# Two decoder layers on one core: statistics' matmuls at fixed places of TensorE's order, six convolution taps emitted per chunk, freer transposes, and x's second half on another queue

## The chip, the core and the metric

The kernel runs on one NeuronCore of a Trainium2 chip. The metric is the time of one execution in device microseconds. A core has five engines that each work through a list of instructions in order and meet at semaphores: TensorE (PE, matrix products), VectorE (DVE), ScalarE (ACT), GpSimd (POOL) and SyncE (SP), which here only issues DMAs. TensorE and the others exchange results through PSUM, whose tiles are few.

## What is computed

Two layers; each runs a convolution branch and an attention branch on the same x (256 rows of 1024), merges them and normalizes. Shortened from the reference (with 256 rows and blocks of 256 the attention is plain causal attention):

```python
def hybrid_layer(x, w_in, b_in, conv_w, conv_b, cln_g, cln_b, w_pw2,
                 w_proj_a, w_proj_b, w_out, ln_g, ln_b, positions):
    u = x @ w_in + b_in
    a_val, a_glu, a_z, q, k, v, b_z, g_a, g_b = jnp.split(u, SPLIT_POINTS, axis=-1)
    h_a = conformer_conv(a_val, a_glu, conv_w, conv_b, cln_g, cln_b, w_pw2) * jax.nn.silu(a_z)
    y_a = h_a @ w_proj_a
    ...
    o = moba_attention(rope(q), rope(k), v)
    y_b = (o * jax.nn.silu(b_z)) @ w_proj_b
    merged = jax.nn.sigmoid(g_a) * y_a + jax.nn.sigmoid(g_b) * y_b
    out = merged @ w_out
    return layer_norm(DEEPNORM_ALPHA * x + out, ln_g, ln_b)

def conformer_conv(...):
    h = a_val * jax.nn.sigmoid(a_glu)
    # causal, one filter of 31 taps for each channel
    h = lax.conv_general_dilated(h, conv_w, ...) + conv_b
    h = jax.nn.silu(layer_norm(h, cln_g, cln_b))
    return h @ w_pw2
```

## The kernel before

**Weights and chunks.** The weights of a layer come in blocks of 256 columns (1 MB each) in the order of STREAM: V, then A_GLU and A_VAL in turn, B_Z, then MID (Q, K and G_A in turn for j = 0 to 3, then four times G_B), A_Z, PB, PW2, PA and WO, four blocks each. `load_w` issues their DMAs on SP's queue. `split_w` cuts a block into a rounded part hi (ScalarE, L120) and a rest lo (mostly GpSimd, L124). `gemm_a` computes two chunks of 128 output columns for a block: for each, eight matmuls of 512 columns with hi against x's own hi and lo parts (L176), and eight of 256 columns with lo (L174). A chunk's result lies in a PSUM tile of the pool `mmp`, which has three; ScalarE adds the bias to one half (L182) and VectorE adds the halves (L187). For Q and K the second chunk is added into the first one's tile, and VectorE's rope (L430 to L434) reads that tile, whose last reader is the addition L434.

**Convolution.** Its 31 taps for each of eight channel groups are 248 instructions a layer on VectorE, each a multiply and add into a PSUM accumulator (L373 for the first tap, L377 for the others). They wait in a list; after each chunk, `background(nconv[0])` emits NCV of them, with a lower priority, into the scheduler, which decides where they stand in VectorE's order. After the last tap of a group the group is added into a fold (L382).

**The convolution's norm.** `cln_mu` is a matmul of ones with the fold (cmu, L536), then VectorE subtracts the mean (L539) and ScalarE squares (L540). `cln_var` folds the squares (L527 to L529), has a matmul of ones (cvar, L545) and builds the factor r; `cln_b` makes from it, group by group, the input hc of PW2 (L558 to L562). `hook_az` calls cln_mu after chunk CM = 3 of A_Z and cln_var after chunk CV = 7; `ev_pb` calls cln_b along the chunks of PB, by the table CB.

**The boundary of the layers.** `part` is the product with WO, and V's in layer 1; `out_ln` normalizes 128 rows with `rstd`, whose VectorE instructions on 128x1 values are L221 to L225; `out_tr` transposes the new x (L652, two groups of four, one PSUM bank each) and splits it into hi (L654, ScalarE) and lo (L655, VectorE). The hook in `part` puts the first `out_tr` between the last matmuls of WO.

**What sets the order.** DMA queues run in order of issue. The Tile scheduler orders each engine's instructions by dependencies and priorities. Under `manual_schedule` TensorE's order is that of the code; this is so in MID, and from the last part of WO in layer 0 to the end of V in layer 1.

Of the kernel before, what the change touches and what calls it, by code (L numbers as in the profile page):

```python
# [10 lines left out]
F32 = mybir.dt.float32  # L11
# [3 lines left out]
AF = mybir.ActivationFunctionType  # L15
ALU = mybir.AluOpType
# [6 lines left out]
P = 128  # L23
KT = D // P
# [6 lines left out]
CW = 256  # L31
# [1 line left out]
EARLY = 6  # L33
NH2 = 2
CM = 3.0
CV = 7.0
CB = [[], [0], [1, 2], [3, 4], [5, 6], [7], [], []]
KE = 7
KN = 5
# [4 lines left out]
HP = 0  # L44
LATE = 150
LAG = 3
NCV = 4

A_VAL, A_GLU, A_Z, Q, K, V, B_Z, G_A, G_B, PW2, PA, PB, WO = range(13)
ORDER = [(V, j) for j in range(4)]  # L50
# [20 lines left out]
def decoder_trunk(ctx: ExitStack, tc: tile.TileContext, a, out):  # L71
    nc = tc.nc
# [3 lines left out]
    rawp = ctx.enter_context(tc.tile_pool(name="rawp", bufs=3))  # L76
# [11 lines left out]
    def u_f32(name, shape=(P, KT, S)):  # L88
        return unit.tile(list(shape), F32, tag="u", name=name)

    def u_pair(name):

        both = pair.tile([P, KT, 2, S], F32R, tag="p", name=name)
        return both[:, :, 0, :], both[:, :, 1, :], both

    def load_w(i):
        l, b, j = STREAM[i]
        raw = rawp.tile([P, KT, CW], F32, tag="raw", name=f"raw{i}")
        n = {1: 4, 2: 2}.get(i, 1)
        for q in range(n):  # L100
            ks = slice(q * KT // n, (q + 1) * KT // n)
            nc.sync.dma_start(out=raw[:, ks, :], in_=a["w"][i, :, ks, :])
        return raw

    W = {}
    raws = {}
# [43 lines left out]

    nconv = [NCV]
    pcs = [None]
# [43 lines left out]
    def wide(w):  # L196

        return w.rearrange("p (k h) c -> p k (h c)", h=2)

    def part(o, lhs, w, t, kh, late_x=False, cols=slice(0, 512), ks=range(4), hook=None):  # L200
        wh, wl = (wide(n) for n in w)
        xh, xl = lhs
        ts = slice(t * P, t * P + P)
        if late_x:
            seq = [(k, q) for q in (0, 2, 1) for k in ks]
        else:
            seq = [(k, q) for k in ks for q in (0, 1)] + [(k, 2) for k in ks]
        for n, (k, q) in enumerate(seq):
            kk = 4 * kh + k
            nc.tensor.matmul(o, (xl if q == 1 else xh)[:, kk, ts], (wl if q == 2 else wh)[:, k, cols],  # L210
                             start=(kk == 0 and n == 0), stop=(kh == 1 and n == len(seq) - 1))
            if hook is not None and n == 7:
                hook()

    def rstd(mv, name, fast):
        v = small.tile([P, 1], F32, tag="var", name="var" + name)
        y = small.tile([P, 1], F32, tag="ry", name="ry" + name)
        u = small.tile([P, 1], F32, tag="ru", name="ru" + name)
        if not fast:
            nc.scalar.activation(u, mv, AF.Sqrt, bias=eps)  # L220
            nc.vector.tensor_scalar(v, mv, EPS, None, op0=ALU.add)  # L221
            nc.vector.reciprocal(y, u)
            nc.vector.scalar_tensor_tensor(u, y, v, y, op0=ALU.mult, op1=ALU.mult)
            nc.vector.tensor_scalar(u, u, -0.5, 1.5, op0=ALU.mult, op1=ALU.add)
            nc.vector.tensor_tensor(y, y, u, op=ALU.mult)  # L225
            return y
        nc.gpsimd.tensor_scalar(v, mv, EPS, -0.5, op0=ALU.add, op1=ALU.mult)
        nc.scalar.activation(u, mv, AF.Sqrt, bias=eps)
        nc.vector.reciprocal(y, u)
        nc.scalar.activation(u, y, AF.Square)  # L230
        nc.scalar.activation(u, u, AF.Identity, scale=v, bias=oneh)
        nc.scalar.activation(y, y, AF.Copy, scale=u)
        return y

    xh, xl, xp = u_pair("x0")
    xf = u_f32("xf0")
    raw = rawp.tile([P, KT, CW], F32, tag="raw", name="raw0")
# [12 lines left out]
    for k in range(4):  # L250
        nc.sync.dma_start(out=raw4[:, k, :], in_=a["w"][0, :, 2 * k : 2 * k + 2, :])
        nc.scalar.dma_start(out=xf[:, k, :], in_=a["xT"][:, k, :])
    for k in (4, 6):
        nc.scalar.dma_start(out=xf[:, k : k + 2, :], in_=a["xT"][:, k : k + 2, :])

    def split_x(k0, k1):
        ks = slice(k0, k1)
# [4 lines left out]
    for k in range(NH2, 4):  # L262
        ks = slice(2 * k, 2 * k + 2)
# [35 lines left out]
    for l in range(DEPTH):  # L299
# [6 lines left out]
        x, xb = (xh, xl), xp  # L306

        v = u_f32(f"v{l}", (P, 2, D))
# [4 lines left out]
        if l == 0:  # L313
            for n in range(2):
# [5 lines left out]
                for kh in range(2):  # L320
                    w = next_w()
# [21 lines left out]
            ident, ones, mask, rt = load_consts()  # L343
# [74 lines left out]
        og, ol, op_ = u_pair(f"og{l}")  # L418
# [90 lines left out]
        for n, (b, j) in enumerate(MID):  # L509
            def hook(c, n=n):  # L510
                with tc.high_priority(offset=HP):
                    for f, p in plan.get(2 * n + c, []):
                        f(p)
# [28 lines left out]
        def cln_var():  # L542
            f = fold(cln["sq"], cln["sq"])
            vp = cvp.tile([P, 2, S], F32, tag="cv", name=f"cvar{l}")
            nc.tensor.matmul(vp[:, 0, :], ones, f, start=True, stop=True)  # L545
            u = tmp.tile([P, S], F32, tag="g", bufs=2, name=f"cu{l}")
            y = vp[:, 1, :]
            nc.scalar.activation(u, vp[:, 0, :], AF.Sqrt, bias=eps)
            nc.vector.reciprocal(y, u)
            nc.scalar.activation(u, y, AF.Square)  # L550
            nc.vector.tensor_scalar(vp[:, 0, :], vp[:, 0, :], EPS, None, op0=ALU.add)
            nc.vector.scalar_tensor_tensor(u, u, -0.5, vp[:, 0, :], op0=ALU.mult, op1=ALU.mult)
            nc.vector.scalar_tensor_tensor(y, u, 1.5, y, op0=ALU.add, op1=ALU.mult)
            cln["r"] = y
# [8 lines left out]

        def ev_pb(ct, o):
            nc.vector.scalar_tensor_tensor(gb[:, ct, :], gb[:, ct, :], 1.0, o, op0=ALU.add, op1=ALU.mult)
            if ct == 0:
                hc.extend(u_pair(f"hc{l}"))
            for q in CB[ct]:
                cln_b(q)

        def hook_az(c, j):
            if 2 * j + c == CM:
                background(len(conv_ops))
                cln_mu()
            if 2 * j + c == CV:
                cln_var()

        for j in range(4):
            gemm_a(xb, ev_az, lambda c, j=j: hook_az(c, j))
        for j in range(4):  # L580
            gemm_a(op_, ev_pb)

        rows = load_rows(l)
        if l == 0:
# [25 lines left out]
        xn = xs  # L610
        if not last:
            xh, xl, xp = u_pair(f"x{l + 1}")
# [33 lines left out]

        def out_tr(t):
            xt = sp.tile([P, 2, 512], F32, tag="s", name=f"xt{l}_{t}")
            for g in range(2):
                tp = xt[:, g, :].rearrange("p (i q) -> p i q", i=4)  # L650
                for i in range(4):
                    nc.tensor.transpose(tp[:, i, :], xn[:, t, 512 * g + i * P : 512 * g + i * P + P], ident)  # L652
                xd = xh[:, 4 * g : 4 * g + 4, t * P : t * P + P]
                nc.scalar.activation(xd, tp, AF.Copy)  # L654
                nc.vector.tensor_tensor(xl[:, 4 * g : 4 * g + 4, t * P : t * P + P], tp, xd.bitcast(F32),  # L655
                                        op=ALU.subtract)

        ws = hold_w(4)
        for i, (t, n, kh) in enumerate(((0, 0, 0), (1, 0, 0), (0, 0, 1), (0, 1, 0), (0, 1, 1),
# [88 lines left out]
```

## Time and profile before

| | |
|---|---|
| time, median of three runs | 666.62 us (664.55 to 667.56) |
| time of the profiled execution | 663.44 us |
| its span (first to last instruction) | 661.7 us |
| mean granted TensorE clock | 0.993 |
| busy TensorE, VectorE | 636.9 us, 498.4 us |
| busy GpSimd, ScalarE | 484.9 us, 437.7 us |

The span is what the profiler's rows cover; the execution's own time holds it and 1.7 us around it. Busy time is summed over the whole span, while the stages load the engines very differently, so that it doesn't tell which engine is waited for in a stage. The trace's views do: waits (who was idle until whom), timeline (instructions in order of time, with the idle time just ahead of them in brackets) and windows (busy time by stretch).

### The profile page before, as it was taken

To read this page: it belongs to the slowest core of one execution; us is meant where nothing else is said; L and a number is where in the kernel's file an instruction comes from. 1 tells how busy PE (TensorE), PEld (TensorE's weight loads), DVE (VectorE), ACT (ScalarE), POOL (GpSimd) and SP (SyncE) were. 2 spreads that over 40 slices of the span, in tenths; PEclk is the share of its full clock that TensorE was granted. 3 is DMA by queue.
4 is the path that set the end of the run, shared out by engine and by line. 5 is a ranking of instruction groups with operands and counts; after the bars stand their busy time and mean duration, and the time that the engine had idled before them with its cause. 6 is when DMAs were issued, how large, how long until landed. Compare 5 with 4: busy or idle time off the path is not lost.

```text
span 661.7 us, 10603 instructions
## 1 busy us (share of the span) xinstructions
PE 636.9 (96%) x3662; PEld 544.3 (82%) x3662; DVE 498.4 (75%) x1130; ACT 437.7 (66%) x1017; POOL 484.9 (73%) x385
## 2 busy tenths in 40 slices
PE   7999999999999889999799999999999998999995
PEld 5788888888888778988678888888888887889884
DVE  3658989998998775456740789999999988654556
ACT  4765665887878687666516565758787875875640
POOL 0189999776667679989606998997677677799850
PEclk9999999999999999999989999999999999999999
DMA  8965555534443536555631565453443353355511
GB/s 270 371 251 194 189 192 192 190 128 135 149 165 128 204 131 230 200 191 191 254 128 64 199 222 216 158 215 137 163 157 128 127 189 131 128 202 206 181 50 63
DMA packets 19190, 116.06 MB, mean 175 GB/s; under 512 B 2112, under 2 KB 3392, under 8 KB 6208
## 3 DMA queue, kind: packets, MB, share of 16 engines
q1 hardware_dynamic: 18272, 114.33, 48.1%
q10 hardware_dynamic: 864, 1.05, 0.5%
q8 instruction: 29, 0.48, 0.3%
q14 instruction: 25, 0.20, 0.1%
HBM read 114.32 MB, written 1.05 MB: 174 GB/s over the span
## 4 chain that ended last, share of the span: by engine, by line
PE 85%; DVE 6%; DMA 3%; ACT 3%; POOL 1%; issue 1%; SPq 0%; DVEq 0%; ACTq 0%
PE mm L176 45%; PE mm L174 23%; PE wo L210 4%; DMA raw<-w 3%; PE v L210 3%; PE s L446 2%; PE mm L171 2%; PE v L336 2%; DVE fold L382 2%; PE tb L486 1%; ACT hi L120 1%; POOL lo L124 1%; DVE lo L124 1%; ACT sq L540 1%; PE ta L473 1%; PE tb L474 1%
## 5 line engine op out<-in xcount | busy, mean ns | idle before, releaser
L124 POOL TENSOR_TENSOR lo<-raw,hi 128x512 fp32r<-128x512 f32 x380 | 484.5, 1317 | 152.5 <-ACT hi L120 117.3
L176 PE MATMUL mm<-x,hi 128*128 128x512 f32 x1024 | 262.3, 394 | 0.4 <-ACT bz L411 0.4
L120 ACT ACTIVATE hi<-raw 128x512 fp32r<-128x512 f32 x412 | 234.7, 627 | 18.5 <-DMA raw<-w 12.3
L176 PEld LDWEIGHTS mm<-x,hi 128*128 128x128 f32 x1024 | 184.2, 189 | 35.6 <-issue 2.1
L377 DVE SCALAR_TENSOR_TENSOR cv<-h,pc,cv 128x256 f32<-128x256 f32 x464 | 195.3, 479 | 0.2
L174 PEld LDWEIGHTS mm<-x,lo 128*128 128x128 f32 x1024 | 139.7, 190 | 11.3
L174 PE MATMUL mm<-x,lo 128*128 128x256 f32 x1024 | 148.1, 284 | 0.0
L187 DVE TENSOR_TENSOR mm<-mm,lw 128x256 f32<-128x256 f32 x172 | 73.5, 429 | 83.0 <-ACT lw L182 49.7
L182 ACT ACTIVATE lw<-mm,pc 128x256 f32<-128x256 f32 x128 | 61.1, 478 | 87.9 <-PE mm L176 87.8
L176 PE MATMUL mm<-og,hi 128*128 128x512 f32 x128 | 32.8, 395 | 0.0
L210 PE MATMUL wo<-hi,mg 128*128 128x512 f32 (+1 forms) x144 | 32.6, 367 | 0.0
L176 PE MATMUL mm<-ah,hi 128*128 128x512 f32 x128 | 32.4, 392 | 0.0
L210 PEld LDWEIGHTS wo<-hi,mg 128*128 128x128 f32 x144 | 25.2, 189 | 5.1 <-DVE mg L603 0.7
L124 DVE TENSOR_TENSOR lo<-raw,hi 128x512 fp32r<-128x512 f32 x32 | 25.5, 844 | 3.9 <-ACT hi L120 3.9
L184 ACT ACTIVATE lw<-mm 128x256 f32<-128x256 f32 x44 | 16.8, 387 | 16.8 <-PE mm L176 16.4
L176 PEld LDWEIGHTS mm<-og,hi 128*128 128x128 f32 x128 | 23.1, 189 | 4.2
L176 PEld LDWEIGHTS mm<-ah,hi 128*128 128x128 f32 x128 | 23.0, 189 | 4.0
L176 PE MATMUL mm<-hc,hi 128*128 128x512 f32 x96 | 24.4, 392 | 0.0
L176 PEld LDWEIGHTS mm<-hc,hi 128*128 128x128 f32 x96 | 17.4, 189 | 3.1
L210 PE MATMUL wo<-lo,mg 128*128 128x512 f32 (+1 forms) x72 | 18.6, 381 | 0.0
L174 PEld LDWEIGHTS mm<-ah,lo 128*128 128x128 f32 x128 | 17.5, 190 | 1.2
L174 PEld LDWEIGHTS mm<-og,lo 128*128 128x128 f32 x128 | 17.5, 190 | 1.2
(133 smaller groups left out, 719.9 us busy)
## 6 DMA issues: line engine op xcount, KB each, us to landing
raw<-w SPq DMA_DIRECT2D x101, 1024.0 KB, 4.8
raw<-w SPq DMA_DIRECT2D x8, 256.0 KB, 5.6
rows<-pr SPq DMA_DIRECT2D x4, 512.0 KB, 5.2
raw<-w SPq DMA_DIRECT2D x2, 512.0 KB, 7.2
xs<-x SPq DMA_DIRECT2D x1, 1024.0 KB, 7.2
out<-xs SPq DMA_DIRECT2D x3, 256.0 KB, 2.0
xf<-xT ACTq DMA_DIRECT2D x4, 128.0 KB, 5.8
xf<-xT ACTq DMA_DIRECT2D x2, 256.0 KB, 5.3
```

The costliest lines, as they stand in the source:

```text
L120: nc.scalar.activation(hi[:, ks, :], raw[:, ks, :], AF.Copy)
L124: eng.tensor_tensor(lo[:, ks, :], raw[:, ks, :], hi[:, ks, :].bitcast(F32), op=ALU.subtract)
L171: nc.tensor.matmul(ps[:, 0, :], (wl if q == 2 else wh)[:, k, cs], both[:, k, int(q == 1), :], start=(n == 0), stop=(n == len(seq) - 1))
L174: nc.tensor.matmul(ps[:, 0, :], wl[:, k, cs], both[:, k, 0, :], start=False, stop=False)
L176: nc.tensor.matmul(ps, wh[:, k, cs], both[:, k, :, :], start=(n == 0), stop=(k == KT - 1))
L182: nc.scalar.activation(t, low, AF.Identity, bias=pcs[0][:, b * KT + ct : b * KT + ct + 1])
L184: nc.scalar.activation(t, low, AF.Copy)
L187: nc.vector.tensor_tensor(kept[:, c if b in (Q, K) else 0, :], o, t, op=ALU.add)
L210: nc.tensor.matmul(o, (xl if q == 1 else xh)[:, kk, ts], (wl if q == 2 else wh)[:, k, cols], start=(kk == 0 and n == 0), stop=(kh == 1 and ...
L336: nc.tensor.matmul(o[t], (xl if r == 1 else xh)[:, kk, ts], (wl if r == 2 else wh)[:, k, :], start=(kk == 0 and r == 0), stop=(kk == 7 and ...
L377: r = nc.vector.scalar_tensor_tensor(dst, src, w, acc[:, c, :], op0=ALU.mult, op1=ALU.add)
L382: nc.vector.tensor_tensor(f, dst if ct > 1 else h[:, 0, TAPS - 1 :], f if ct > 1 else dst, op=ALU.add)
```

## The change

- CV becomes 0 and is now compared in `ev_pb`: `cln_var` is called after the first chunk of PB and no longer after the last chunk of A_Z.
- NCV becomes 6: six taps are emitted after each chunk.
- The chunks of A_Z and PB are under `manual_schedule`, so that cmu and cvar stand where the code calls them.
- The hook in `part` comes one matmul later (n == 8).
- In `rstd`, a scalar_tensor_tensor and a tensor_tensor on 128x1 become tensor_scalar with 128x1 scalars.
- In `out_tr`, the transposes of the second bank are declared independent of the readers of the first bank.
- The last four of x's eight column blocks are loaded on SP's queue between the pieces of the second weight block, and no longer on ACT's queue.

```diff
@@ -33,7 +33,7 @@
 EARLY = 6
 NH2 = 2
 CM = 3.0
-CV = 7.0
+CV = 0
 CB = [[], [0], [1, 2], [3, 4], [5, 6], [7], [], []]
 KE = 7
 KN = 5
@@ -44,7 +44,7 @@
 HP = 0
 LATE = 150
 LAG = 3
-NCV = 4
+NCV = 6
 
 A_VAL, A_GLU, A_Z, Q, K, V, B_Z, G_A, G_B, PW2, PA, PB, WO = range(13)
 ORDER = [(V, j) for j in range(4)]
@@ -96,7 +96,7 @@
     def load_w(i):
         l, b, j = STREAM[i]
         raw = rawp.tile([P, KT, CW], F32, tag="raw", name=f"raw{i}")
-        n = {1: 4, 2: 2}.get(i, 1)
+        n = 2 if i == 2 else 1
         for q in range(n):
             ks = slice(q * KT // n, (q + 1) * KT // n)
             nc.sync.dma_start(out=raw[:, ks, :], in_=a["w"][i, :, ks, :])
@@ -209,7 +209,7 @@
             kk = 4 * kh + k
             nc.tensor.matmul(o, (xl if q == 1 else xh)[:, kk, ts], (wl if q == 2 else wh)[:, k, cols],
                              start=(kk == 0 and n == 0), stop=(kh == 1 and n == len(seq) - 1))
-            if hook is not None and n == 7:
+            if hook is not None and n == 8:
                 hook()
 
     def rstd(mv, name, fast):
@@ -220,9 +220,9 @@
             nc.scalar.activation(u, mv, AF.Sqrt, bias=eps)
             nc.vector.tensor_scalar(v, mv, EPS, None, op0=ALU.add)
             nc.vector.reciprocal(y, u)
-            nc.vector.scalar_tensor_tensor(u, y, v, y, op0=ALU.mult, op1=ALU.mult)
+            nc.vector.tensor_scalar(u, y, v, y, op0=ALU.mult, op1=ALU.mult)
             nc.vector.tensor_scalar(u, u, -0.5, 1.5, op0=ALU.mult, op1=ALU.add)
-            nc.vector.tensor_tensor(y, y, u, op=ALU.mult)
+            nc.vector.tensor_scalar(y, y, u, None, op0=ALU.mult)
             return y
         nc.gpsimd.tensor_scalar(v, mv, EPS, -0.5, op0=ALU.add, op1=ALU.mult)
         nc.scalar.activation(u, mv, AF.Sqrt, bias=eps)
@@ -250,8 +250,12 @@
     for k in range(4):
         nc.sync.dma_start(out=raw4[:, k, :], in_=a["w"][0, :, 2 * k : 2 * k + 2, :])
         nc.scalar.dma_start(out=xf[:, k, :], in_=a["xT"][:, k, :])
-    for k in (4, 6):
-        nc.scalar.dma_start(out=xf[:, k : k + 2, :], in_=a["xT"][:, k : k + 2, :])
+    raws[1] = rawp.tile([P, KT, CW], F32, tag="raw", name="raw1")
+    for k in range(4):
+        ks = slice(2 * k, 2 * k + 2)
+        if k % 2 == 0:
+            nc.sync.dma_start(out=xf[:, k + 4 : k + 6, :], in_=a["xT"][:, k + 4 : k + 6, :])
+        nc.sync.dma_start(out=raws[1][:, ks, :], in_=a["w"][1, :, ks, :])
 
     def split_x(k0, k1):
         ks = slice(k0, k1)
@@ -563,8 +567,9 @@
 
         def ev_pb(ct, o):
             nc.vector.scalar_tensor_tensor(gb[:, ct, :], gb[:, ct, :], 1.0, o, op0=ALU.add, op1=ALU.mult)
-            if ct == 0:
+            if ct == CV:
                 hc.extend(u_pair(f"hc{l}"))
+                cln_var()
             for q in CB[ct]:
                 cln_b(q)
 
@@ -572,13 +577,13 @@
             if 2 * j + c == CM:
                 background(len(conv_ops))
                 cln_mu()
-            if 2 * j + c == CV:
-                cln_var()
 
         for j in range(4):
-            gemm_a(xb, ev_az, lambda c, j=j: hook_az(c, j))
+            with tc.manual_schedule(engines={mybir.EngineType.PE}):
+                gemm_a(xb, ev_az, lambda c, j=j: hook_az(c, j))
         for j in range(4):
-            gemm_a(op_, ev_pb)
+            with tc.manual_schedule(engines={mybir.EngineType.PE}):
+                gemm_a(op_, ev_pb)
 
         rows = load_rows(l)
         if l == 0:
@@ -646,14 +651,19 @@
 
         def out_tr(t):
             xt = sp.tile([P, 2, 512], F32, tag="s", name=f"xt{l}_{t}")
+            before = []
             for g in range(2):
                 tp = xt[:, g, :].rearrange("p (i q) -> p i q", i=4)
                 for i in range(4):
-                    nc.tensor.transpose(tp[:, i, :], xn[:, t, 512 * g + i * P : 512 * g + i * P + P], ident)
+                    r = nc.tensor.transpose(tp[:, i, :], xn[:, t, 512 * g + i * P : 512 * g + i * P + P], ident)
+                    for q in before:
+                        tc.declare_no_dep(r.ins, q, reason="another bank")
                 xd = xh[:, 4 * g : 4 * g + 4, t * P : t * P + P]
-                nc.scalar.activation(xd, tp, AF.Copy)
-                nc.vector.tensor_tensor(xl[:, 4 * g : 4 * g + 4, t * P : t * P + P], tp, xd.bitcast(F32),
-                                        op=ALU.subtract)
+                r = nc.scalar.activation(xd, tp, AF.Copy)
+                before.append(r.ins)
+                r = nc.vector.tensor_tensor(xl[:, 4 * g : 4 * g + 4, t * P : t * P + P], tp, xd.bitcast(F32),
+                                            op=ALU.subtract)
+                before.append(r.ins)
 
         ws = hold_w(4)
         for i, (t, n, kh) in enumerate(((0, 0, 0), (1, 0, 0), (0, 0, 1), (0, 1, 0), (0, 1, 1),
```

What stands where, from the built orders. A name is the tile of the code with its layer or weight block, and a number of its own at the end; the lines of the changed kernel are up to 6 higher.

VectorE in MID of layer 0, from the addition of K3's first chunk (mm27_0, block 27 of the stream) to the end of its rope; cv is the convolution's accumulator, s and nm belong to the attention. Before:

```order
L187 TENSOR_TENSOR mm27_0_1969<-mm27_0_1969,lw27_0_1986 128x256
L377 SCALAR_TENSOR_TENSOR cv0_2_1551<-h_161,pc0_181,cv0_2_1551 128x256 x3
L452 TENSOR_TENSOR s0_5_2014<-s0_5_2014,mask_333 128x2x256
L377 SCALAR_TENSOR_TENSOR cv0_2_1551<-h_161,pc0_181,cv0_2_1551 128x256
L453 TENSOR_REDUCE nm0_5_2019<-s0_5_2014 128x2
L187 TENSOR_TENSOR mm27_0_1969<-mm27_1_1993,lw27_1_2044 128x256
L454 TENSOR_REDUCE nm0_5_2019<-s0_5_2014 128x2
L430 TENSOR_TENSOR u_0_4_3_2047<-mm27_0_1969,rt_335 128x512
L432 TENSOR_TENSOR mm27_0_1969<-mm27_0_1969,rt_335 128x512
L431 STREAM_SHUFFLE t2_0_4_3_2048<-u_0_4_3_2047 128x512
L377 SCALAR_TENSOR_TENSOR cv0_2_1551<-h_161,pc0_181,cv0_2_1551 128x256
L434 TENSOR_TENSOR r_0_4_3_2052<-mm27_0_1969,t2_0_4_3_2048 128x512
```

Now:

```order
L187 TENSOR_TENSOR mm27_0_2052<-mm27_0_2052,lw27_0_2069 128x256
L497 TENSOR_TENSOR og0_1120<-tb0_3_1947,og0_1120 128x256
L381 SCALAR_TENSOR_TENSOR cv0_3_1616<-h_166,pc0_181,cv0_3_1616 128x256 x6
L456 TENSOR_TENSOR s0_5_2099<-s0_5_2099,mask_333 128x2x256
L381 SCALAR_TENSOR_TENSOR cv0_3_1616<-h_166,pc0_181,cv0_3_1616 128x256
L187 TENSOR_TENSOR mm27_0_2052<-mm27_1_2078,lw27_1_2129 128x256
L457 TENSOR_REDUCE nm0_5_2104<-s0_5_2099 128x2
L434 TENSOR_TENSOR u_0_4_3_2132<-mm27_0_2052,rt_335 128x512
L436 TENSOR_TENSOR mm27_0_2052<-mm27_0_2052,rt_335 128x512
L435 STREAM_SHUFFLE t2_0_4_3_2133<-u_0_4_3_2132 128x512
L381 SCALAR_TENSOR_TENSOR cv0_3_1616<-h_166,pc0_181,cv0_3_1616 128x256
L438 TENSOR_TENSOR r_0_4_3_2137<-mm27_0_2052,t2_0_4_3_2133 128x512
```

From the first of these additions to the end of the rope stand five taps before (3, 1 and 1) and eight now (6, 1 and 1); they belong to the third pair of channel groups before (cv0_2) and to the fourth and last pair now (cv0_3).

TensorE around the convolution's norm in layer 0; mm33 to mm36 are A_Z, mm37 is the first block of PB. Before:

```order
L174 MATMUL mm35_1_2686<-x0_94,lo34_2499 128x256 x3
L536 MATMUL cmu0_2647<-fold0_949,ones_329 128x256
L174 MATMUL mm35_1_2686<-x0_94,lo34_2499 128x256 x5
L176 MATMUL mm35_1_2686<-x0_94,hi34_2498 128x512
L176 MATMUL mm36_0_2719<-x0_94,hi35_2560 128x512 x7
L174 MATMUL mm36_0_2719<-x0_94,lo35_2561 128x256 x8
L176 MATMUL mm36_0_2719<-x0_94,hi35_2560 128x512
L176 MATMUL mm36_1_2740<-x0_94,hi35_2560 128x512 x7
L174 MATMUL mm36_1_2740<-x0_94,lo35_2561 128x256 x8
L176 MATMUL mm36_1_2740<-x0_94,hi35_2560 128x512
L545 MATMUL cvar0_2764<-sq0_2646,ones_329 128x256
```

Now, around cmu:

```order
L174 MATMUL mm34_1_2630<-x0_94,lo33_2466 128x256 x8
L176 MATMUL mm34_1_2630<-x0_94,hi33_2465 128x512
L540 MATMUL cmu0_2652<-fold0_819,ones_329 128x256
L176 MATMUL mm35_0_2673<-x0_94,hi34_2542 128x512 x7
L174 MATMUL mm35_0_2673<-x0_94,lo34_2543 128x256 x8
```

and around cvar:

```order
L176 MATMUL mm37_0_2787<-og0_1120,hi36_2663 128x512 x7
L174 MATMUL mm37_0_2787<-og0_1120,lo36_2664 128x256 x8
L176 MATMUL mm37_0_2787<-og0_1120,hi36_2663 128x512
L549 MATMUL cvar0_2812<-sq0_2651,ones_329 128x256
L176 MATMUL mm37_1_2821<-og0_1120,hi36_2663 128x512 x7
L174 MATMUL mm37_1_2821<-og0_1120,lo36_2664 128x256 x8
```

cmu stood inside the sixth chunk of A_Z and now stands behind the fourth; cvar stood between A_Z and PB and now stands behind the first chunk of PB, five chunks after cmu.

TensorE at the boundary of the layers; wo is WO's output, xt the transposed x, v1 layer 1's V. Before:

```order
L210 MATMUL wo0_1_512_3683<-lo50_3527,mg0_3280 128x512 x4
L210 MATMUL wo0_1_512_3683<-hi51_3538,mg0_3280 128x512 x8
L652 MATMUL xt0_0_3718<-ident_331,xs0_3033 128x128 x8
L210 MATMUL wo0_1_512_3683<-lo51_3539,mg0_3280 128x512 x4
L210 MATMUL v1_0_0_3756<-hi52_3576,x1_3521 128x512 x4
L210 MATMUL v1_0_0_3756<-lo52_3577,x1_3521 128x512 x4
```

Now:

```order
L210 MATMUL wo0_1_512_3707<-lo50_3551,mg0_3304 128x512 x4
L210 MATMUL wo0_1_512_3707<-hi51_3562,mg0_3304 128x512 x8
L210 MATMUL wo0_1_512_3707<-lo51_3563,mg0_3304 128x512
L658 MATMUL xt0_0_3743<-ident_331,xs0_3057 128x128 x8
L210 MATMUL wo0_1_512_3707<-lo51_3563,mg0_3304 128x512 x3
L210 MATMUL v1_0_0_3780<-hi52_3600,x1_3545 128x512 x4
L210 MATMUL v1_0_0_3780<-lo52_3601,x1_3545 128x512 x4
```

One matmul of WO's last block has moved ahead of the eight transposes, three stand behind them.

## Rows read from the trace of the kernel before

**Rows 1.** The page's first part, engines' busy us, share and instructions.
```profile
PE 636.9 (96%) x3662; PEld 544.3 (82%) x3662; DVE 498.4 (75%) x1130; ACT 437.7 (66%) x1017; POOL 484.9 (73%) x385
```

**Rows 2.** Waits of TensorE: us in total, times, longest.
```profile
PE cmu L536 <- DVE fold L382: 3.9, 2, 2.0
PE cvar L545 <- DVE sq L529: 3.7, 2, 1.8
PE xt L652 <- DVE x L655: 2.8, 2, 1.4
...
PE xt L652 <- DVE xs L643: 2.3, 1, 2.3
PE v L336 <- ACT hi L120: 0.6, 1, 0.6
```

**Rows 3.** Windows, attention of layer 0: stretch, us, busy us of each engine.
```profile
126.90:177.30 50.40, 50.40 (x323) 41.78 (x323) 46.78 (x111) 40.06 (x114) 34.41 (x28) 1.00 0.42 147
```

**Rows 4.** Timeline of VectorE in MID: start, us, engine, line, work.
```profile
158.49 2.04 DVE L377 SCALAR_TENSOR_TENSOR cv<-h,pc,cv 128x256 f32<-128x256 f32 x5
...
176.61 0.69 DVE L434 TENSOR_TENSOR r<-mm,t 128x512 f32<-128x512 f32 x1
...
182.21 1.47 DVE L382 TENSOR_TENSOR fold<-h,fold 128x256 f32<-128x256 f32 x1
...
184.21 0.91 DVE L382 TENSOR_TENSOR fold<-h,fold 128x256 f32<-128x256 f32 x1
```

**Rows 5.** Timeline of TensorE in MID.
```profile
179.37 2.00 PE L176 MATMUL mm<-x,hi 128*128 128x512 f32 x8
```

**Rows 6.** Timeline, A_Z to PW2 of layer 0; brackets: idle before, releaser.
```profile
224.12 2.91 DVE L382 TENSOR_TENSOR fold<-h,fold 128x256 f32<-128x256 f32 x2
...
227.09 0.70 PE L536 MATMUL cmu<-fold,ones 128*128 128x256 f32 x2 [1.95 <-DVE fold L382]
...
236.02 0.70 PE L545 MATMUL cvar<-sq,ones 128*128 128x256 f32 x2 [1.83 <-DVE sq L529]
...
255.97 0.42 DVE L562 TENSOR_TENSOR hc<-z,hc 128x256 fp32r<-128x256 f32 x1 [0.55 <-ACT hc L561]
...
258.90 1.77 PE L176 MATMUL mm<-hc,hi 128*128 128x512 f32 x7
```

**Rows 7.** Timeline, boundary of the layers.
```profile
322.75 8.67 POOL L124 TENSOR_TENSOR lo<-raw,hi 128x512 fp32r<-128x512 f32 x7 [0.78 <-ACT hi L120]
...
324.31 1.01 DVE L223 SCALAR_TENSOR_TENSOR ruy<-ryy,vary 128x1 f32<-128x1 f32 x1
...
325.58 0.13 DVE L224 TENSOR_SCALAR ruy<-ruy 128x1 f32<-128x1 f32 x1
325.75 0.79 DVE L225 TENSOR_TENSOR ryy<-ryy,ruy 128x1 f32<-128x1 f32 x1
326.57 1.41 DVE L643 SCALAR_TENSOR_TENSOR xs<-wo,ryy,rows 128x512 f32<-128x512 f32 x2
...
327.38 0.91 PE L652 MATMUL xt<-ident,xs 128*128 128x128 f32 x4 [2.30 <-DVE xs L643]
...
329.70 1.11 PE L652 MATMUL xt<-ident,xs 128*128 128x128 f32 x4 [1.41 <-DVE x L655]
...
335.16 1.99 PE L210 MATMUL v<-hi,x 128*128 128x512 f32 x8
...
335.95 0.22 DVE L223 SCALAR_TENSOR_TENSOR ruy<-ryy,vary 128x1 f32<-128x1 f32 x1
...
336.40 0.16 DVE L225 TENSOR_TENSOR ryy<-ryy,ruy 128x1 f32<-128x1 f32 x1
```

**Rows 8.** Windows with the granted clock (1.00 is full) after the busy times.
```profile
226.00:236.00 10.00, 7.11 (x40) 6.06 (x40) 8.03 (x8) 5.56 (x10) 5.57 (x5) 1.00 0.56 210
...
327.90:334.70 6.80, 5.39 (x16) 4.08 (x15) 3.50 (x8) 1.49 (x3) 3.52 (x3) 0.52 0.63 249
```

**Rows 9.** Timeline, start of the kernel.
```profile
10.04 0.61 ACT L258 ACTIVATE x<-xf 128x512 fp32r<-128x512 f32 x1
```

## The prediction

> **What bounds the kernel now.** The page's first part comes first: TensorE is the busiest engine, 636.9 of 661.7 us [rows 1], and VectorE's average of 75% says little, because its stages differ. So the next view is TensorE's list of waits [rows 2]. It is short: 3.9 us for the convolution's mean (cmu, behind the last fold), 3.7 us for its variance (cvar), both twice, once a layer; and 2.3 + 2.8 us at the boundary of the layers, where TensorE transposes the new x. That is what a change of order can give back. The third view asks who is nearly late where TensorE does not wait. In 126.9 to 177.3 us, inside the attention stretch (the MID weights) of layer 0, TensorE is busy all 50.40 us, and VectorE 46.78 [rows 3]: there VectorE has 3.62 us of idle time and no more. A kernel in which TensorE is full everywhere loses one for one whatever VectorE is late by in such a stretch.
>
> **Six taps a chunk.** The order of VectorE's instructions is the same up to chunk 32 (chunks counted from the first of A_GLU, so that MID is 24 to 55). I counted the built order from the addition L187 of chunk 32 to the last rope addition of K3 (row L434 before, L438 after): 44 taps before, 78 after; of the other instructions 46 and 47, two folds more and one reduction fewer. A tap costs its distance to the next one: five in a row take 2.04 us with 0.48 for one, so (2.04 - 0.48) / 4 = 0.39 us [rows 4]. 34 taps are 13.3 us; the two folds that move ahead of this point took 1.47 and 0.91 us, 2.4 together [rows 4]; I subtract nothing for the reduction. VectorE then needs 46.8 + 13.3 + 2.4 = 62.5 us of work where it had 50.4 us of time, and can finish the rope of K3 no sooner than 126.9 + 62.5 = 189.4 us.
>
> Who waits for it: K3's two chunks are added into one PSUM tile that the rope reads to its end; of the three mm tiles this is the one that the first chunk of G_B takes. Before, the rope ends at 176.61 + 0.69 = 177.3 us [rows 4], and that chunk starts with the second of eight matmuls that begin at 179.37, at 179.6 us [rows 5]: 2.3 us to spare. After, it has to wait until 189.4, **9.8 us**. Behind that matmul stands all of TensorE's work, so the loss is final; it will appear in pieces at several chunks from about 39 on. The two bounds: if folds cost nothing extra and every idle moment is filled, 126.9 + 46.8 + 13.3 - 179.6 = 7.4; if the 3.6 us of idle stay idle, 9.8 + 3.6 = 13.4. I take 9.8, because a late VectorE finds its inputs ready. The counts are the same in layer 1, so the term is 19.6 us (14.8 to 26.8). After chunk 52 no taps are left and nothing of this can be won back: TensorE is full in every later stage too.
>
> **cmu and cvar at fixed places.** With the taps done eight chunks earlier, the fold (two folds of 2.91 us in all end just before cmu [rows 6]) lies far ahead of cmu, which now stands right behind the fourth A_Z chunk: its 3.9 us go. cvar came 236.02 - 227.09 = 8.9 us after cmu, of which TensorE waited 1.83 [rows 6]; now five chunks stand between the two. Eight 512-column matmuls take 1.99 us [rows 7], and a chunk has those and eight of half the width, so five are about 14 us against a chain of 8.9: the 3.7 us go as well. Gain 7.6 us (bounds 0 and 7.6: two waits can't give more). The cover: what follows the variance starts one chunk of PB later. Today the last hc piece begins at 255.97, 20.0 us after cvar, and PW2 begins 258.90 and asks for the last piece 2.5 us later, at the end of its first chunk [rows 6]. Measured from cvar, PW2 comes a chunk (2.8 us) sooner after the change: last piece ready at 20.4, asked for at 22.6. It just fits; beyond 2 us of delay there PW2 waits.
>
> **The boundary.** Three edits work on 327 to 336 us. In rstd, two 128x1 instructions with tensor operands took 1.01 and 0.79 us while GpSimd was splitting weights, and 0.22 and 0.16 us a little later, when it was not [rows 7]; a TENSOR_SCALAR of the same size, L224, took 0.13 under the same GpSimd work. Both become TENSOR_SCALAR, so the chain gets 0.86 + 0.64 = 1.5 us shorter. [...] Then the first transposes can start at 327.38 - 1.5 = 325.9 instead of 327.38, and the second four no longer wait for the first bank's readers but for the second half of xs, 0.7 us later (half of 1.41), so all are done by about 327.2; the three matmuls that were moved behind them cost nothing, one stands ahead of them instead. 11 matmuls then lie before the eight v matmuls that began at 335.16: at (1.99 - 0.39) / 7 = 0.23 us each 2.5 us, so these begin at 329.7, 5.4 us sooner. [...] The second boundary wait of 1.4 (half of the 2.8 [rows 2]) goes too. Gain 5.4 + 1.4 = **6.8 us** (3.5 if the clock falls all the same; 1.5 more is lost if the new rstd is held up).
>
> **x's second half on the weights' queue.** It may remove the 0.6 us wait for the split behind x's late pieces [rows 2], and puts one x piece of 0.61 us [rows 9] ahead of the one that the first split matmuls need: -0.6 to +0.6, taken as 0. In MID TensorE's transposes of p stand a chunk later in places; no wait is there today, and the 2.3 us to spare cover it; beyond that they would wait at their own cost.
>
> **Sum.** Span 661.7, execution 663.4 us. 663.4 - 7.6 - 6.8 + 19.6 = 668.6. The median of the runs shown, 666.6, is 3.2 above this execution, so on that scale **671.8**, which I round to 672. About 0.5% (3.3 us) is what a measurement of this kernel can tell from no change.
>
> **Rivals.**
> A, faster: VectorE finds the room. All gains come (14.4 us), and MID loses under 5.5 us a layer instead of 9.8; then the median is below 666.6 - 14.4 + 11 = 663.2, and with no loss 652. For it: VectorE has 3.6 us idle and 2.3 to spare in that stretch. Against: that is 5.9 us against 15.7 of new work. It decides at 11.4 us of added work, that is, a tap spacing of about 0.26 us or less, and the rows show 0.39. Chance 0.17.
> B: the clock falls in MID. The waits there are scattered like those at the boundary, and a stretch of 6.8 us at half speed costs up to 3.3. Against: the single wait of 1.95 at cmu left the clock at 1.00 [rows 8], and while VectorE is the later engine a slower TensorE is partly hidden. One to two such stretches a layer: +3 to +12, 675 to 684. Chance 0.2.
> C: MID as forecast, but part of the gains stays out: PW2 waits 1 to 2 us a layer for hc, or rstd stays held (1.5) and the clock falls at the boundary (3.3): 674 to 679. Chance 0.1.
> D, the change of taps does nothing: VectorE's order could have been the same; the built order excludes it.
>
> **How the numbers follow.** Forecast 0.53, with a range of its own of 667 to 679 from the bounds of MID. Range 659 to 682: it leaves out the faster half of A and the far end of B. Slower by over 0.5% is above 669.9: B, C and six tenths of the forecast, 0.61; the same (663.3 to 669.9): the rest of the forecast and a little of A, 0.23; faster 0.16.
>
> **What would show it.** Right: TensorE waits for VectorE's rope and L187 (and ScalarE's gates behind it) inside MID, 15 to 27 us in both layers, VectorE close to 100% busy over chunks 39 to 51, no wait at cmu, cvar and the second transposes, the two rstd instructions at 0.2 us or less beside GpSimd. Wrong: VectorE's taps in MID closer than 0.3 us, TensorE full in MID, or a granted clock near 0.5 in MID or still at the boundary.

## The result, and the profile after

The changed kernel takes 692.28 us (median of four runs, 690.62 to 694.49), the kernel before, run beside it, 666.13; the ratio is 1.0395, with a 95% interval of 1.0355 to 1.0435. It was forecast to be slower, by 0.8% and not by 4%. Its profiled execution has a span of 691.3 us, 29.6 more than before, and a mean granted clock of 0.968 (0.993 before).

The first part of the page (the row that answers to [rows 1]):

```profile
PE 651.9 (94%) x3662; PEld 552.2 (80%) x3662; DVE 486.0 (70%) x1130; ACT 440.3 (64%) x1017; POOL 486.0 (70%) x385
```

TensorE executes the same 3662 matmuls, and is busy 15.0 us longer with them. Its waits (they answer to [rows 2]; us in total, times, longest):

```profile
PE ta L476 <- ACT p L467: 13.9, 8, 2.8
PE tb L478 <- DVE og L497: 10.8, 6, 2.3
...
PE mm L176 <- DVE r L438: 1.4, 4, 0.4
PE mm L176 <- DVE mm L187: 0.9, 4, 0.2
PE xt L658 <- DVE xs L648: 0.7, 1, 0.7
```

cmu, cvar and the second transposes of the boundary are gone from the list. In their place stand 27.0 us in the attention stretch (13.9 + 10.8 + 1.4 + 0.9), and only 2.3 of these at the rope and the additions, where the prediction had them. The rest is at the transposes of p: the first ones into ta wait for ScalarE's last step of the softmax, and the first into tb for a PSUM tile that the head pair before still holds, until VectorE has made its og. Windows of layer 0 (busy us of TensorE, its weight loads, VectorE, ScalarE and GpSimd, then the granted clock, the DMA share and GB/s):

```profile
126.00:216.00 90.00, 76.27 (x415) 60.28 (x416) 76.55 (x188) 53.60 (x151) 45.64 (x37) 0.89 0.30 106
140.00:150.00 10.00, 9.96 (x49) 8.03 (x50) 7.56 (x19) 3.10 (x7) 1.91 (x2) 0.71 0.26 105
170.00:180.00 10.00, 8.32 (x44) 6.81 (x44) 7.95 (x19) 2.15 (x6) 0.53 (x1) 0.67 0.32 106
200.00:210.00 10.00, 8.25 (x38) 6.59 (x38) 7.53 (x20) 3.77 (x11) 2.50 (x3) 0.66 0.48 184
```

The first answers to [rows 3] and shows that VectorE is not full: 76.55 of 90 us. The other three are the stretches behind three pairs of long waits; the clock in them is 0.66 to 0.71 on average. Read in steps of 0.5 us, in the first of them it is 0.50 up to 145.5 us and 1.00 from 146.0 on. The first of these pairs in the timeline:

```profile
136.12 0.18 DVE L465 RECIPROCAL rc<-sm 128x4 f32<-128x4 f32 x1 [0.72 <-ACT s L463]
136.22 1.63 DVE L381 SCALAR_TENSOR_TENSOR cv<-h,pc,cv 128x256 f32<-128x256 f32 x4
...
136.76 0.38 ACT L467 ACTIVATE p<-s,rc 128x128 f32<-128x128 f32 x1
...
137.19 0.33 PE L476 MATMUL ta<-ident,p 128*128 128x128 f32 x1 [1.11 <-ACT p L467]
...
137.76 0.48 DVE L495 SCALAR_TENSOR_TENSOR tb<-tb,pc,bz 128x256 f32<-128x256 f32 x1
137.97 1.19 ACT L120 ACTIVATE hi<-raw 128x512 fp32r<-128x512 f32 x2
...
139.01 0.43 ACT L496 ACTIVATE og<-tb 128x256 fp32r<-128x256 f32 x1
...
139.47 0.42 DVE L497 TENSOR_TENSOR og<-tb,og 128x256 fp32r<-128x256 f32 x1 [0.50 <-ACT og L496]
...
140.04 0.45 PE L478 MATMUL tb<-ident,p 128*128 128x128 f32 x1 [2.15 <-DVE og L497]
...
141.06 1.65 PE L450 MATMUL s<-r,r 64*128 64x256 f32 x8
...
157.30 0.92 PE L450 MATMUL s<-r,r 64*128 64x256 f32 x8
```

Four taps (1.63 us) stand on VectorE between the reciprocal and the attention's L495; behind L495, ScalarE's copy of og comes behind two pieces of a weight split (1.19), then L497; tb waits 2.15 us for it; ta had waited 1.11 just before, and 0.7 us of transposes lie between the two waits. The scores that follow take 1.65 us for eight matmuls; later, at full clock, the same eight take 0.92 (the last line). Layer 1 has three such pairs as well; at each of the six the clock was granted at 0.50, for 6.8 us at five and for 3.4 at one.

Around the convolution's norm the change does what was forecast. The rows that answer to [rows 6] (cvar, last piece of hc, first matmuls of PW2):

```profile
257.79 0.59 PE L549 MATMUL cvar<-sq,ones 128*128 128x256 f32 x2
...
277.07 0.43 DVE L566 TENSOR_TENSOR hc<-z,hc 128x256 fp32r<-128x256 f32 x1 [0.82 <-ACT hc L565]
...
277.77 1.77 PE L176 MATMUL mm<-hc,hi 128*128 128x512 f32 x7
```

cvar doesn't wait, the last piece is ready 19.7 us behind it (277.07 + 0.43 - 257.79), and PW2, which asks for it some 22.5 us behind cvar, doesn't wait either. The boundary (it answers to [rows 7]):

```profile
341.77 7.53 POOL L124 TENSOR_TENSOR lo<-raw,hi 128x512 fp32r<-128x512 f32 x6 [0.77 <-ACT hi L120]
...
343.33 0.26 DVE L223 TENSOR_SCALAR ruy<-ryy,vary 128x1 f32<-128x1 f32 x1
...
344.01 0.21 DVE L225 TENSOR_SCALAR ryy<-ryy,ruy 128x1 f32<-128x1 f32 x1
...
345.07 1.31 PE L658 MATMUL xt<-ident,xs 128*128 128x128 f32 x8 [0.73 <-DVE xs L648]
```

The two instructions of rstd take 0.26 and 0.21 us beside a busy GpSimd, where 1.01 and 0.79 stood; one wait of 0.73 is left of three, and the granted clock is 1.00 there.

### The profile page after: what moved, and what is told of

Its sections match the earlier page's. It is cut to its first block, busy times and chain, and to the rows that moved or that the text cites. A ratio compares the mean times of both kernels' runs of the same rounds, so it can differ in the third digit from the quotient of the medians.

```text
span 691.3 us, 10609 instructions
## 1 busy us (share of the span) xinstructions
PE 651.9 (94%) x3662; PEld 552.2 (80%) x3662; DVE 486.0 (70%) x1130; ACT 440.3 (64%) x1017; POOL 486.0 (70%) x385
## 4 chain that ended last, share of the span: by engine, by line
PE 86%; ACT 5%; DVE 4%; DMA 3%; POOL 1%; issue 1%; DVEq 0%; ACTq 0%
PE mm L176 44%; PE mm L174 24%; PE wo L210 3%; PE v L210 3%; PE v L340 3%; PE s L450 3%; ACT hi L120 2%; PE mm L171 2%; DMA raw<-w 1%; DMA xf<-xT 1%; PE tb L490 1%; POOL lo L124 1%; ACT s L463 1%; PE tb L478 1%; PE ta L476 1%
## 5 line engine op out<-in xcount | busy, mean ns | idle before, releaser
L176 PE MATMUL mm<-x,hi 128*128 128x512 f32 x1024 | 267.0, 397 | 2.3 <-DVE r L438 1.4
L187 DVE TENSOR_TENSOR mm<-mm,lw 128x256 f32<-128x256 f32 x172 | 73.7, 428 | 116.5 <-ACT lw L182 84.9
L174 PEld LDWEIGHTS mm<-x,lo 128*128 128x128 f32 x1024 | 143.5, 196 | 11.9 <-issue 1.3
L174 PE MATMUL mm<-x,lo 128*128 128x256 f32 x1024 | 151.9, 290 | 0.0
L176 PE MATMUL mm<-hc,hi 128*128 128x512 f32 x96 | 24.4, 392 | 0.0
L476 PE MATMUL ta<-ident,p 128*128 128x128 f32 x32 | 10.4, 324 | 13.9 <-ACT p L467 13.9
L478 PE MATMUL tb<-ident,p 128*128 128x128 f32 x32 | 10.4, 324 | 10.8 <-DVE og L497 10.8
L481 ACT ACTIVATE pa<-ta 128x512 f32<-128x512 f32 x16 | 9.6, 602 | 16.4 <-PE ta L477 16.3
```

The lines of the kernel that those rows point to most:

```text
L174: nc.tensor.matmul(ps[:, 0, :], wl[:, k, cs], both[:, k, 0, :], start=False, stop=False)
L176: nc.tensor.matmul(ps, wh[:, k, cs], both[:, k, :, :], start=(n == 0), stop=(k == KT - 1))
L187: nc.vector.tensor_tensor(kept[:, c if b in (Q, K) else 0, :], o, t, op=ALU.add)
L476: nc.tensor.transpose(ta[:, e, :P], p0[:, e, :], ident)
L478: nc.tensor.transpose(tb[:, e, :], p1[:, e, P:], ident)
```

## The experiments

Times are medians; each is compared with runs of the kernel before on the same chip.

**Six taps alone, in the kernel before.**

```diff
-NCV = 4
+NCV = 6
```

> The kernel before with six taps a chunk and nothing else. Theory 1 (the taps alone make the loss: VectorE's steps of the attention come late behind them, TensorE waits at the transposes of p and the clock falls there): about 699 us, that is the 692.3 of the full change with the boundary's 6.8 us not gained; waits at the transposes of p about 25 us, no wait at cmu. Rival 2 (the loss comes from the fixed places of TensorE's order in A_Z and PB, or from x's other queue): 659 to 666 us, no waits in the attention stretch.

703.53 us, ratio 1.0559 (1.0524 to 1.0594), clock 0.966. The waits in the attention stretch are those of the full change:

```profile
PE ta L472 <- ACT p L463: 14.0, 8, 2.8
PE tb L474 <- DVE og L493: 11.0, 6, 2.3
```

So this one number makes the whole loss, and the rest of the change earns 11 us of it back. Rival 2 falls.

**The full change with four taps.**

```diff
-NCV = 6
+NCV = 4
```

> The full change with four taps a chunk again. Theory 1: the attention stretch is as before, the boundary's gain of about 6.8 us stays, cvar's 3.7 may go, cmu still waits about 3.9: 655 to 660 us, mean clock back at 0.99. Rival 2: still 685 to 695 us.

652.88 us, ratio 0.9802 (0.9776 to 0.9828), clock 0.995. No wait is left in the attention stretch; cmu waits as before:

```profile
PE cmu L540 <- DVE fold L386: 3.9, 2, 2.0
...
PE xt L658 <- DVE xs L648: 0.8, 1, 0.8
PE v L340 <- DVE x L263: 0.5, 1, 0.5
PE mm L176 <- ACT bz L415: 0.3, 1, 0.3
```

**Four taps, and the mean's matmul after the sixth chunk of A_Z.**

```diff
-CM = 3.0
+CM = 5.0
-NCV = 6
+NCV = 4
```

> As the one before it, and the mean's matmul called after the sixth chunk of A_Z and not after the fourth. Theory 1: the fold is ready by then, so cmu's 3.9 us go too; cvar then comes three chunks (about 8.4 us) behind cmu against a chain of 8.9, so it waits about 0.5 a layer: 651 to 655 us. Rival 2: 685 to 695.

649.96 us, ratio 0.9758 (0.9739 to 0.9778), clock 0.997. cmu still waits 2.3 of 3.9 us, cvar no longer; the time is 1 us below what was expected. This is the lowest median of all versions.

**The boundary's three edits alone, in the kernel before.** Edit: the lines of the diff in `part` (n == 8), `rstd` and `out_tr`.

> The kernel before with the three edits at the boundary alone (tensor_scalar in rstd, the hook one matmul later, the second bank's transposes free). By the prediction's sum 6.8 us less, 659.3, with the two 128x1 instructions at 0.2 us or less beside GpSimd and no stretch at half clock; 662.6 if the clock falls there all the same; 664 or more if GpSimd still holds the tensor_scalar up.

657.40 us, ratio 0.9868 (0.9842 to 0.9893): 8.4 us gained by the medians, 6.0 between the spans of the two profiled executions (661.7 and 655.7). In the window that [rows 8] shows at a clock of 0.52, TensorE is now busy throughout at 1.00 (first line):

```profile
327.90:334.70 6.80, 6.80 (x33) 5.64 (x32) 6.22 (x15) 1.48 (x4) 4.49 (x4) 1.00 0.65 199
228.00:233.00 5.00, 5.00 (x23) 4.22 (x22) 3.35 (x4) 3.57 (x6) 1.29 (x1) 0.66 0.95 340
```

The 128x1 TENSOR_SCALARs took 0.26 and 0.21 us. The boundary's own gain by the traces is 4.4 us of waits (5.1 to 0.7) and 3.3 of clock. The 8.4 us can't be put down to it alone: cvar's waits fell too, from 3.7 to 1.0 us, though nothing was edited there (why was not followed up), and the clock fell behind cmu's wait of 1.96 us in both layers (second line, layer 0), where it stayed up in the trace of [rows 8]. That trace has a mean clock of 0.993; the runs of the kernel before beside this one had 0.987 to 0.990.

**A dose of taps.** Six are emitted, but with a priority further back in the scheduler's order (LATE), which leaves fewer in the attention stretch.

```diff
-LATE = 150
+LATE = 250
```

and 220, 180 in its place.

> The full change with the taps' priority 250 places back and not 150: between the addition of chunk 32 and the end of K3's rope now stand 55 taps (44 with four a chunk, 78 in the full change). Theory P (the prediction's sum: VectorE has 3.6 us idle and 2.3 to spare, each tap costs 0.39): 11 taps and two folds are 6.7 us against 5.9, so 0.8 us late a layer; without cmu's wait the base is 652.9 - 3.9 = 649, so 650 to 651 us. Theory W (what is late is the softmax's way through VectorE to the transposes of p, and TensorE's clock falls behind it from the first wait on): 660 or more.

> The same with 220 places: 62 taps. Theory P: 3.5 us late a layer, 656 us, clock 0.99. Theory W: between the 649 of no waits and the 692 of the full change by the share of taps, about 672, with a clock below 0.985.

> The same with 180 places: 70 taps. Theory P: 6.7 us late a layer, 662 us. Theory W: about 682, with waits at the transposes of p and a clock of about 0.975.

668.39 us (ratio 1.0052, 1.0031 to 1.0072), 680.95 (1.0247, 1.0230 to 1.0264) and 685.68 (1.0311, 1.0291 to 1.0332). The waits of the first:

```profile
PE tb L478 <- DVE og L497: 6.4, 4, 2.0
PE ta L476 <- ACT p L467: 3.8, 2, 1.9
PE mm L176 <- DVE r L438: 2.8, 2, 1.4
```

Added work in the table is measured: VectorE's busy time from the addition of chunk 32 to the end of K3's rope, above that of the kernel before (46.82 us a layer). The waits are those of the whole attention stretch, some of which stand behind that rope.

| kernel | taps from chunk 32 to K3's rope | added work of VectorE up to K3's rope, both layers | TensorE's waits in the attention stretch | TensorE busy | clock | time |
|---|---|---|---|---|---|---|
| four taps, mean later | 44 | 0 | 0 | 633.5 | 0.997 | 649.96 |
| LATE = 250 | 55 | 8.7 | 13.5 | 641.4 | 0.988 | 668.39 |
| LATE = 220 | 62 | 14.4 | 21.1 | 645.6 | 0.979 | 680.95 |
| LATE = 180 | 70 | 19.0 | 24.8 | 644.7 | 0.978 | 685.68 |
| full change | 78 | 27.8 | 27.0 | 651.9 | 0.968 | 692.28 |

Both theories miss on the way. Theory P subtracts 5.9 us of room a layer, and no dose shows it: the waits are longer than the added work at the three smaller doses and about as long at the largest. Theory W has the places and the falling clock right, but the cost does not follow the share of taps: the first 18 taps a layer (with the two folds) cost 31.0 of the 42.3 us, the last 16 the rest.

**The waits filled with dead work.** In `att_trans`, for the head pairs 1, 3 and 5:

```diff
+            def fill(o):
+                for _ in range(20 if p in (1, 3, 5) else 0):
+                    nc.tensor.matmul(o, warm, warm, start=True, stop=True)
...
+                if e == 0:
+                    fill(ta[:, 0, :P])
                 nc.tensor.transpose(ta[:, e, :P], p0[:, e, :], ident)
                 nc.tensor.transpose(ta[:, e, P:], p1[:, e, :P], ident)
+                if e == 0:
+                    fill(ta[:, 1, :P])
                 nc.tensor.transpose(tb[:, e, :], p1[:, e, P:], ident)
```

> The full change with 20 dead matmuls of 128 columns ahead of the first transposes into ta and again ahead of the first into tb, for the heads' pairs 1, 3 and 5 of each layer, the places of the long waits; what they write is overwritten. They ask whether the clock's fall is on the path. If it is (theory C): the waits shrink by what fills them, the clock stays up and the time falls by up to 15 us, to 677 to 685. If the chain through VectorE and ScalarE sets the pace anyway (theory D): the clock is up and the time stays at 690 to 697.

685.39 us, ratio 1.0305 (1.0282 to 1.0329), 6.9 below the full change; the clock is 0.989. The group of the added matmuls, and the waits:

```profile
L477 PE MATMUL ta<-warm 128*128 128x128 bf16 x240 | 15.4, 219 | 0.0
```

```profile
PE ta L482 <- ACT p L467: 7.0, 4, 1.8
PE tb L486 <- DVE og L505: 4.7, 6, 1.1
```

TensorE is busy 658.2 us, 15.4 of them with dead work; the other matmuls take 642.8, 9.1 less than in the full change. The waits fell by 14.6 us, about what fills them, and the span fell by 6.9 (6.0 by the ratios, each against the kernel before on its own chip): the clock is on the path, for two thirds to three quarters of what it gives back. The time is 0.4 us above theory C's range and 4.6 below theory D's. No fall is left at the filled places; three are left behind single waits of 1.75 us at the pairs 2 and 4, which were not filled (mean clock 0.96 in 126 to 213 us, 0.98 in 460 to 565). VectorE's order moved a little as well (83 taps up to K3's rope), which by the dose above should cost rather than gain.

**The transposes one chunk later, with the 78 taps in place.**

```diff
-L1, L2, L3 = 2.5, 5.5, 7.0
+L1, L2, L3 = 2.5, 6.5, 8.0
...
-                        plan.setdefault(at + d, []).append((f, p))
+                        plan.setdefault(min(at + d, 31.0), []).append((f, p))
```

> The full change with the transposes of p and the product with v called one chunk later (L2 = 6.5, L3 = 8.0, the last at the end of MID); VectorE's 78 taps between chunk 32's addition and K3's rope stay. Theory W (the softmax's way to the transposes has only 1 to 1.5 us to spare, and that is what the taps use up): a chunk more of spare takes most of the 24.7 us of waits at ta and tb away, and the clock's falls with them: 650 to 662 us. Theory P (VectorE has too much work for the stretch, wherever it is asked for): the waits move to the rope and the additions, 18 to 20 us in both layers, 668 us with the clock up, 680 or more if it falls.

677.79 us, ratio 1.0194 (1.0171 to 1.0217), 14.5 below the full change. That is far above theory W's 650 to 662 and between theory P's 668 (clock up) and 680 (clock falls), with a mean clock of 0.985; but the waits are not where theory P had them. They are:

```profile
PE tb L478 <- DVE og L497: 12.8, 6, 3.2
PE s L450 <- ACT p L468: 5.6, 4, 1.4
PE mm L176 <- DVE mm L187: 4.4, 4, 1.8
```

Its windows of the attention stretch of layer 0, and of 5 us behind the longest wait (3.17 us, up to 156.98):

```profile
126.00:213.00 87.00, 75.39 (x457) 62.06 (x458) 81.31 (x199) 57.58 (x162) 49.64 (x41) 0.96 0.33 119
157.00:162.00 5.00, 5.00 (x22) 4.29 (x23) 5.00 (x13) 4.31 (x15) 0.95 (x1) 0.66 0.55 197
```

The waits at ta are gone and others stand in their place: og, the scores (whose one PSUM tile is held until p is made) and L187, 23.5 us with 0.7 of small ones, against 27.0. VectorE is now busy 81.31 of 87 us. The edit gives a chunk more to p's path, but none to og's, since the product with v moved along with the transposes; so ta's waits went and tb's stayed. The spare of a path decides where TensorE waits, while the sum of the waits fell by 3.5 us only. TensorE is busy 641.0 us, 10.9 less than in the full change: most of the 14.5 us are clock. Four falls are left, each behind a single wait (3.17 or 2.75 us; in layer 0 the clock is 0.83 in 156 to 166 us and 0.85 in 186 to 196).

**x's second half alone, in the kernel before.** Edit: the lines of the diff at `load_w` and at the loads of x.

> The kernel before with x's second half on the weights' queue alone. By the prediction's bounds -0.6 to +0.6 us: 664.5 to 666.5, no verdict. If the first split matmuls wait for the x piece that now stands ahead of theirs, up to 1.5 us more.

662.99 us, ratio 0.9971 (0.9955 to 0.9987): 1.5 us gained. The two waits of 0.6 and 0.3 us at the start are gone. The 1.5 us are not shown to be the edit's alone: cvar's waits were 1.2 us shorter too, without an edit, and the waits at the start vary, from 0.9 to 1.5 us in the three versions that leave the start as it was, and from 0 to 1.0 in those that have this edit.

**Two more ways to finish the convolution early.** LATE = 300 with six taps and CM = 4; five taps with CM = 5.

> Six taps with a priority 300 places back and the mean's matmul after the fifth chunk of A_Z: up to K3's rope the 44 taps of four a chunk, 7 to 13 more behind it, and the convolution done some two chunks earlier. If the last three head pairs' transposes have the same spare as the others: no wait at cmu and some at ta and tb, 649 to 656 us, so no clear gain over the 650.0 of four taps with the mean later.

> Five taps emitted a chunk, the rest of the full change, and the mean's matmul after the sixth chunk of A_Z: up to K3's rope the same 44 taps as with four, 5 to 6 more behind it, the convolution done one chunk earlier. The 2.3 us of waits at cmu that the 650.0 us version has left should go; if each microsecond of added work on VectorE in the attention stretch is a microsecond of TensorE's waiting, 2.2 us a layer come back at ta and tb: 648 to 652 us, no clear gain.

651.42 us (ratio 0.9799, 0.9773 to 0.9824) and 650.33 (0.9787, 0.9761 to 0.9813): no faster than four taps with the mean later. cmu's wait is gone in both, and tb's is there, of the first:

```profile
PE tb L478 <- DVE og L497: 3.9, 4, 1.0
```

and of the second:

```profile
PE tb L478 <- DVE og L497: 2.0, 2, 1.0
```

Even the 5 to 6 more taps a layer behind K3's rope cost 1.0 us of waiting a layer, about half of what they work (0.39 us each).

## Why the prediction was right and wrong

**Right:** the sign, the cause (the taps), and the gains. cmu's and cvar's 7.6 us went in full. The boundary's 6.8 came as 7.7 by the traces (4.4 of waits, 3.3 of clock). x's queue alone gave 1.5, outside the bounds of 0.6; what of it belongs to the edit stays open. Four taps with the mean later, a version without the taps' loss, is at 650.0, where rival A's end with no loss had 652.

**Wrong, first step: "a late VectorE finds its inputs ready", with the rope as the only place of the waits.** The prediction gave VectorE 62.5 us from chunk 32's addition to the end of K3's rope, all of it work. The window of that stretch in the full change (layer 0), the same with 55 taps (LATE = 250), and VectorE's waits in the first:

```profile
125.80:195.85 70.05, 60.23 (x336) 47.63 (x335) 60.72 (x146) 40.14 (x109) 34.54 (x28) 0.90 0.30 106
126.01:180.73 54.72, 53.13 (x336) 43.58 (x335) 51.18 (x123) 40.48 (x111) 35.83 (x29) 1.00 0.37 135
DVE mm L187 <- ACT lw L182: 5.3, 5, 2.4
DVE rc L465 <- ACT s L463: 3.5, 4, 1.0
```

It took 70.05 us, 60.72 of them busy. So the added work was 13.9 us and not 15.7, and the idle time was not filled: it was 3.6 us of 50.44 before, 3.5 with 55 taps, and 9.3 in the full change. VectorE is late, and then waits for ScalarE's half of a chunk (lw) and for the sums of the softmax. TensorE had stood idle 9.8 us up to the end of the rope (70.05 - 60.23), which is the forecast's number a layer, but by luck: the work was smaller and the idle time larger than in the sum, and the waits were at the transposes. Some 3.9 us a layer more stand behind the rope, so that 27.0 us were measured in both layers for 19.6, just above the upper bound of 26.8.

Why they came at the transposes: each has a spare of its own. In the kernel before (timeline; p of a pair's first head, og of the pair before, and the first transposes into ta and tb):

```profile
145.37 0.36 ACT L463 ACTIVATE p<-s,rc 128x128 f32<-128x128 f32 x1
...
147.03 0.42 DVE L493 TENSOR_TENSOR og<-tb,og 128x256 fp32r<-128x256 f32 x1
...
148.07 0.27 PE L472 MATMUL ta<-ident,p 128*128 128x128 f32 x1
...
148.53 0.27 PE L474 MATMUL tb<-ident,p 128*128 128x128 f32 x1
```

p is ready at 145.73 and used at 148.07, 2.34 us later, about the rope's spare of 2.3 and not the 1 to 1.5 that theory W gave it. og is ready at 147.45, and tb's tile is taken at 148.53, 1.08 us later; that path has less to spare than the rope. Both recur with every head pair: p's spare is 2.1 to 2.8 us at the pairs 1 to 7, og's is 0.83 at pair 4. Nor was VectorE's idle time in the stretch of [rows 3] room. Most of its 3.62 us are these two waits:

```profile
DVE mm L187 <- ACT lw L182: 1.2, 3, 0.5
DVE s L452 <- PE s L446: 1.1, 3, 0.5
```

In such a moment VectorE waits for a step of another engine. That taps put ahead of a step of the attention move the step, and don't use the moment, is how we read the growing idle time and the dose; no run separates it. The expectation of VectorE close to 100% busy (76.55 of 90) failed with it. (The trace has 61 and 62 other instructions in the stretch, not 46 and 47; their difference, which is all the sum uses, is the same.)

**Wrong, second step: the clock at nothing in the sum.** Rival B had the mechanism and priced it at 3 to 12 us. Three falls a layer came, one or two were priced; they came at pairs of waits such as 2.78 and 2.27 us, at a clock of 0.50 for up to 6.8 us each. TensorE's busy time is 15.0 us above before; before had 3.3 of a fall at the boundary in it (6.8 us at 0.52 [rows 8]), which is gone, so that the falls in the attention stretch are 18.3 (against the version without them 651.9 - 633.5 = 18.4). Of its two arguments against, that cmu's single wait of 1.95 us left the clock at 1.00 was luck of that trace: the same wait was followed by a fall in four of its eight profiled cases (none of two in the kernel before; both with the boundary alone, with 0.66 in 228 to 233 us; one of two with four taps and with x's half alone, whose mean clocks are 0.995 and 0.990). That a slower TensorE is partly hidden behind a late VectorE held for a quarter to a third at most: with the dead work in the waits, the rest of what the clock gave back came off the span.

The forecast for the span was 661.7 + 5.2 = 666.9 us, 24.4 below the measured 691.3. The waits in the stretch account for 7.4, the clock there for 18.3; the boundary (4.4 us of waits and 3.3 of clock against 6.8) and the start (about 1) gave some 2 more than forecast, so that 0.7 us stays unassigned.

**Rival C** didn't occur: PW2 waited for nothing. rstd was not held up either: the 128x1 TENSOR_SCALAR took 0.26 us beside GpSimd's work and 0.27 without it (at 351.08, behind the end of that work), where the SCALAR_TENSOR_TENSOR had taken 1.01 and 0.22 [rows 7]. No run shows the 1.5 us that the bounds of the boundary's gain and rival C set aside for a new rstd that is held up. Why the old form took longer beside GpSimd was not shown.

**Open:** with more taps the scheduler also moves matmuls between the transposes in TensorE's order (for some head pairs the pieces into ta and tb stand further apart), so in MID that order is not the code's alone. What that costs by itself was not separated from VectorE's lateness, since the one follows from the other in the built order.

## What to carry to other kernels

Work that is moved into a stretch where another engine is full can cost its own length or more, even if the receiving engine shows 7% idle there: here that idle time consisted of waits inside chains, and it grew. Look at every path that the late engine feeds (here the rope with 2.3 us to spare, p with 2.34 and og with 1.08), and not only at the one that first comes to mind. Waits on TensorE are to be priced with the clock as well: here 27.0 us of them (the longest 2.80) brought 18.4 us of slower matmuls. Try a bundle's parts alone: without the six taps this one gained 13 us, and with them it lost 26.

## What the runs showed of the hardware

- Up to the kernel's last 7 us, the granted clock was below 1.00 in the traces before and after at seven places, the seven pairs of waits on TensorE: 1.11 and 2.15 us, 2.78 and 2.27, 2.80 and 1.06 in layer 0 of the changed kernel, 1.11 and 2.15, 2.79 and 2.14, 2.76 and 1.06 in layer 1, and before, 2.30 and 1.41. Between the waits of a pair lie 0.7 to 0.9 us of transposes. The clock was at 0.50 there, for 6.83 us at six of the pairs and for 3.41 at one; the fall began between 0.6 us ahead of the end of the first wait and 0.5 us behind the end of the second. Behind the other waits of the kernel before (2.73 and 0.60 us at its start, 1.95 and 1.83 in layer 0, 1.41 at the boundary's second transposes, 1.96 and 1.83 in layer 1) it stayed at 1.00. In other versions it fell behind single waits as well: to a mean of 0.66 over 5 us behind 1.96 us (the boundary alone) and behind 3.17 us (the transposes one chunk later).
- A 128x1 TENSOR_SCALAR with a 128x1 scalar took 0.26 us beside GpSimd's splitting of weights and 0.27 without it; the SCALAR_TENSOR_TENSOR in its place 1.01 there and 0.22 without it [rows 7]. So the form that is slightly slower alone is the faster one there.
